# Halves straight out of PSUM, a sink as a scalar, norms in four links, a first FFN block in three pieces

## The chip, the core and the metric

The kernel runs on one core of one Trainium2 chip. The metric is the device time in microseconds of one execution of the whole program. TensorE is called PE here, VectorE DVE, ScalarE ACT, GpSimd POOL; SP issues the DMAs.

## The reference

Two layers of a backbone run over 1024 sample tokens (8 blocks of 128) and one prompt block of 128. Layer 0 mixes tokens by differential attention (8 heads, two maps of 64, 256 cached keys), layer 1 by windowed attention (16 heads in 4 groups, window 128, 256 cached keys, a sink logit per head). After each stands a projection, a norm and a SwiGLU network, D = 1024, 2816 hidden units (22 blocks of 128).

```python
# differential attention, per head
s = einsum(q, k) * HD ** -0.5
p = softmax(s, axis=-1)
a = p[:, :, 0] - lam * p[:, :, 1]
o = einsum(a, v);  o = rmsnorm(o, subln_g) * (1 - lam_init);  y = o @ w_o
# windowed attention: the sink enters maximum and sum
m = maximum(max(s), sk);  e = exp(s - m)
p = e / (sum(e) + exp(sk - m))
# around each network
x = x + gate * rmsnorm(y, g)                     # post_norm
h = rmsnorm(x, g) * (1 + scale) + shift          # pre_norm
y = (silu(h @ w_gate) * (h @ w_up)) @ w_down
```

## The kernel before

Each float32 operand of a product is split in two float32r halves, a rounded high one and the rest as low one, and a product is three matmuls (high by high, high by low, low by high). Inside each stage the program writes the order of PE, DVE, ACT and POOL by hand: what stands first in the code stands first in that engine's queue.

**Differential attention** (some 402 to 806 us) has 32 pairs of token blocks, four for each of 8 heads. The string ROUND says in which order the steps of neighbouring pairs are mixed: a token such as R111 is step R, arguments 1 and 1, of the pair one round back (last digit). S makes scores of map m for block i (two PSUM buffers), R their negative maximum (DVE), E the exponential (ACT), c and C the mix of both maps (DVE, two small instructions and one of 1280 columns), T transposes one of three groups of key blocks into the only PSUM buffer of tag "t", V copies it to SBUF (ACT), P makes the halves (POOL: `pool_round`, then a subtraction), A multiplies by V, X, B, Y bring the result out, W loads and splits a piece of the projection's weights in even rounds. DRAIN is the order after the last round.

**Windowed attention** (1960 to 2235 us) has 32 units. At its start it loads the mask and makes a bfloat16 identity; step S adds the mask by a matmul with that identity, step R takes the maximum and the minimum with the negative sink (line 1026), step E the exponential.

**The projection** (OProj; some 822 to 968 and 2237 to 2366 us) runs over 9 token blocks in the order OORDER = (0, 1, 4, 5, 2, 6, 3, 7, 8). `turn` transposes the attention's result and makes its halves; `proj` does the products, and `norms` sums squares of the result (part 0), does post_norm, the store and the sum of squares of x (part 1) and pre_norm (part 2). `step` lists what is done for which block in each step.

**The first FFN block** (968.7 to 1025.0 and 2366.1 to 2422.5 us) starts while norms still run. The products are a seven-product scheme on halves of the tokens and of the inner dimension (names B11, B21, B22, T1 to T4), made by `Halves` from pairs of token blocks. Part 0 (256 columns) is ready early; part 1 (320 columns) waits for the pairs (2, 6), (3, 7) and the prompt, made by steps listed in `late` between the products of part 0. Weights are split by `prep`: s0 and s1 are sums, h and l halves, u the last pair.

## Time and profile before

| | us |
|---|---|
| median of 3 runs | 3180.54 (3177.97 to 3180.60) |
| the profiled execution | 3179.54 |
| its span | 3177.7 |

Its mean granted clock was 0.982. Over the span PE was busy 3000.0 us (94%), DVE 2070.7 (65%), ACT 1423.8 (45%), POOL 1215.6 (38%). The chain of work that ended last is 68% PE, 13% POOL, 9% DVE, 4% ACT. These are averages over stages with different limits, so rows by stage stand below. An idle time in brackets behind a row is that of its engine before it, and the arrow names what ended it.

### The profile page before, as it was taken

Reading aid. Unit: us, or ns where it says so; the run is one execution under the profiler, and the core shown is the slowest. Engines: PE = TensorE matmul, PEld = TensorE weight load, DVE = VectorE, ACT = ScalarE, POOL = GpSimd, SP = SyncE. Lnnn points to the kernel's source line nnn. Section 1 sums busy time; section 2 is a strip of 40 time slices with the busy share of each in tenths; the row PEclk is TensorE's granted clock in tenths of the full one; section 3 lists DMA queues with packets and bytes.
Section 4 is the critical chain, followed back from the end, with each engine's and each line's share of the span. In section 5 each row is a group of like instructions: output and inputs, shape, how many; then the busy total and the mean of one; then the engine's idle time right before and its main releaser. Section 6 shows DMA issues by size and latency. Waiting matters only on the chain.

```text
span 3177.7 us, 47863 instructions
## 1 busy us (share of the span) xinstructions
PE 3000.0 (94%) x17998; PEld 2637.4 (83%) x17998; DVE 2070.7 (65%) x2849; ACT 1423.8 (45%) x2764; POOL 1215.6 (38%) x1120
## 2 busy tenths in 40 slices
PE   8999989988887999999999998999988999999999
PEld 5888777777776999999888787777768999998887
DVE  6786388888587777753786643999586633334544
ACT  6332267777554333333344323777443333333442
POOL 0453389999312444433000143666213434330000
PEclk9999999999898999999999999999999999999999
DMA  6675543332423343424865454433432322226664
GB/s 214 190 222 190 182 135 115 121 115 85 126 100 98 112 125 110 129 83 150 290 215 193 149 174 126 117 114 102 143 116 75 109 67 79 77 70 214 196 197 142
DMA packets 373807, 442.22 MB, mean 139 GB/s; under 512 B 26804, under 2 KB 295644, under 8 KB 373576
## 3 DMA queue, kind: packets, MB, share of 16 engines
q1 hardware_dynamic: 373576, 439.16, 43.9%
q8 instruction: 142, 2.33, 0.3%
q14 instruction: 89, 0.73, 0.1%
HBM read 335.71 MB, written 103.37 MB: 138 GB/s over the span
## 4 chain that ended last, share of the span: by engine, by line
PE 68%; POOL 13%; DVE 9%; ACT 4%; issue 3%; DMA 1%; SPq 1%; ACTq 0%; DVEq 0%; POOLq 0%
POOL aT L784 7%; PE guX L1516 6%; PE guX L1517 6%; PE guX L1518 6%; PE dacc L1633 6%; PE dacc L1635 6%; PE dacc L1634 6%; POOL aT L110 5%; PE qacc L556 4%; PE qacc L558 4%; PE qacc L557 4%; PE guY L1518 3%; PE guY L1516 3%; PE guY L1517 3%; PE guZ L1516 1%
## 5 line engine op out<-in xcount | busy, mean ns | idle before, releaser
L1633 PE MATMUL dacc<-fh,ahl 128*128 128x512 f32 x792 | 311.4, 393 | 2.4 <-DVE U L1552 2.4
L1635 PE MATMUL dacc<-fh,ahl 128*128 128x512 f32 x792 | 310.3, 392 | 0.0
L1634 PE MATMUL dacc<-fl,ahl 128*128 128x512 f32 x792 | 310.3, 392 | 0.0
L1549 POOL TENSOR_TENSOR sg<-sg,U 128x256 f32<-128x256 f32 x88 | 74.9, 851 | 576.2 <-ACT sg L1548 565.0
L556 PE MATMUL qacc<-whi,hh 128*128 128x512 f32 x648 | 259.3, 400 | 0.0
L558 PE MATMUL qacc<-whi,hl 128*128 128x512 f32 x648 | 254.3, 392 | 0.0
L557 PE MATMUL qacc<-wlo,hh 128*128 128x512 f32 x648 | 253.7, 391 | 0.6 <-DVE wlo L106 0.6
L617 POOL TENSOR_TENSOR qout<-t,t 128x512 f32<-128x512 f32 (+1 forms) x56 | 67.8, 1212 | 485.7 <-DVE vst L587 283.5
L784 POOL TENSOR_TENSOR aT<-a,aT 128x512 fp32r<-128x512 f32 x186 | 237.5, 1277 | 15.5
L1618 DVE TENSOR_TENSOR fl<-fraw,fh 128x1024 fp32r<-128x1024 f32 x132 | 161.7, 1225 | 118.6 <-ACT fh L1617 115.0
L744 DVE TENSOR_REDUCE nm<-S 128x1 f32<-128x1280 f32 x128 | 190.2, 1486 | 50.9 <-PE S L737 50.9
L1617 ACT CAST fh<-fraw 128x1024 fp32r<-128x1024 f32 x132 | 138.4, 1049 | 164.0 <-DMA fraw<-in_w_down_dram 157.4
L737 PE MATMUL S<-K,q 128*128 128x512 f32 (+1 forms) x768 | 184.5, 377 | 13.3 <-ACT e L749 9.2
L266 DVE SCALAR_TENSOR_TENSOR macc<-wmod,sc,macc 128x512 f32<-128x512 f32 x196 | 186.3, 994 | 0.0
L1633 PEld LDWEIGHTS dacc<-fh,ahl 128*128 128x128 f32 x792 | 148.7, 188 | 36.4 <-DVE U L1552 3.3
L1635 PEld LDWEIGHTS dacc<-fh,ahl 128*128 128x128 f32 x792 | 148.7, 188 | 33.5
L578 ACT CAST xT<-tpx 128x512 fp32r<-128x512 f32 x127 | 68.8, 591 | 240.2 <-issue 125.4
L1634 PEld LDWEIGHTS dacc<-fl,ahl 128*128 128x128 f32 x792 | 148.7, 188 | 32.8
L749 ACT ACTIVATE e<-S,nm 128x1280 f32<-128x1280 f32 x128 | 171.6, 1340 | 7.2 <-DVE nm L744 7.1
L737 PEld LDWEIGHTS S<-K,q 128*128 128x128 f32 x768 | 137.5, 193 | 44.3 <-ACT e L749 19.5
L110 POOL TENSOR_SCALAR aT<-a 128x512 fp32r<-128x512 f32 x192 | 154.2, 803 | 24.0 <-ACT a L773 24.0
L1488 DVE TENSOR_TENSOR fl<-fsum,fh 128x1024 fp32r<-128x1024 f32 x84 | 102.4, 1219 | 81.0 <-ACT fh L1486 81.0
(363 smaller groups left out, 9592.2 us busy)
## 6 DMA issues: line engine op xcount, KB each, us to landing
fraw<-in_w_down_dram SPq DMA_DIRECT2D x132, 512.0 KB
wmod<-in_w_mod_dram SPq DMA_DIRECT2D x112, 256.0 KB
araw<-a_d SPq DMA_DIRECT2D x132, 192.0 KB
...
```

Of the source, the lines that this page charges most:

```text
L110: pool.tensor_scalar(out=out, in0=in_, scalar1=1.0, scalar2=0.0, op0=ALU.mult, op1=ALU.add)
L556: pe.matmul(acc, lhsT=xh, rhs=hi[:, a, :], start=(kb == 0), stop=False)
L557: pe.matmul(acc, lhsT=xh, rhs=lo[:, a, :], start=False, stop=False)
L558: pe.matmul(acc, lhsT=xl, rhs=hi[:, a, :], start=False, stop=(kb == KB - 1))
L737: pe.matmul(S[:, j:j + n], lhsT=self.q[:, f, m, i * P:(i + 1) * P], rhs=kv[self.h][0][:, m, j:j + n], start=(f == 0), stop=(f == 1))
L784: (dve if self.last else pool).tensor_tensor(out=lo, in0=x, in1=hi.bitcast(F32), op=ALU.subtract)
L1516: pe.matmul(o, lhsT=hi[:, kb, :], rhs=xh[:, kb, :], start=(first and kb == 0), stop=False, **more)
L1517: pe.matmul(o, lhsT=hi[:, kb, :], rhs=xl[:, kb, :], start=False, stop=False, **more)
L1518: pe.matmul(o, lhsT=lo[:, kb, :], rhs=xh[:, kb, :], start=False, stop=(kb == 3), **more)
L1633: pe.matmul(acc, lhsT=ah, rhs=hi[:, cs], start=(d == 0), stop=False)
L1634: pe.matmul(acc, lhsT=ah, rhs=lo[:, cs], start=False, stop=False)
L1635: pe.matmul(acc, lhsT=al, rhs=hi[:, cs], start=False, stop=(d == NDF - 1))
```

## The change

In the differential attention the second block's third group (g = 2, i = 1, 128x256) gets its high half from ACT's copy out of PSUM and its low half from DVE, which reads PSUM too; the other five groups stay on POOL. ROUND and DRAIN are new orders. The small product of step c becomes a `tensor_scalar` with two pointer scalars. In the windowed attention the minimum with the sink becomes a `tensor_scalar`; mask and identity are made among the small parameters of layer 0. In the projection `turn` makes high halves by ACT and low halves by DVE out of PSUM, and `norms` has four links, of which the last two stand at the start of the step after the next. In the first FFN block part 1 is done as two views, 256 and 64 columns (the prompt); `Halves.first` makes two ACT copies and no DVE copies, and the order of highs and lows is new; the weights of block 1 are prepared from the `late` table, and `fetch` stands at other products. Not shown below: declarations, the pass of rooms from one stage to the next, and the column tables that follow from the views.

```diff
@@ -441,6 +444,10 @@
+        mraw = junk[:, 0:2 * P].rearrange("p (a k) -> p a k", k=P)
+        dma(out=mraw, in_=swa_mask)
+        act.copy(out=mask, in_=mraw)
+        act.copy(out=ident_b, in_=ident)
@@ -753,7 +760,7 @@
-                    dve.scalar_tensor_tensor(out=r, in0=self.s1(i), scalar=neglam, in1=r, op0=ALU.mult, op1=ALU.mult)
+                    dve.tensor_scalar(out=r, in0=r, scalar1=self.s1(i), scalar2=neglam, op0=ALU.mult, op1=ALU.mult)
@@ -767,18 +774,29 @@
-                def step_V(self, g, i):
-                    n = min(4, NKB - 4 * g)
-                    x = self.a32[i, g] = sb.tile([P, 4, P], F32, name="a32", tag="a32", bufs=2)
-                    act.copy(out=x[:, 0:n, :], in_=self.tp[i, g][:, 0:n, :])
-                def step_P(self, g, i):
+                def halves(self, g, i):
...
-                    hi, lo = [self.aT[g][:, f, 0:n, i * P:(i + 1) * P] for f in range(2)]
+                    return [self.aT[g][:, f, 0:n, i * P:(i + 1) * P] for f in range(2)]
+                def step_V(self, g, i):
+                    n = min(4, NKB - 4 * g)
+                    if (g, i) == (2, 1):
+                        act.copy(out=self.halves(g, i)[0], in_=self.tp[i, g][:, 0:n, :])
+                        return
+                    x = self.a32[i, g] = sb.tile([P, 4, P], F32, name="a32", tag="a32", bufs=2)
+                    act.copy(out=x[:, 0:n, :], in_=self.tp[i, g][:, 0:n, :])
+                def step_P(self, g, i):
+                    n = min(4, NKB - 4 * g)
+                    hi, lo = self.halves(g, i)
+                    if (g, i) == (2, 1):
+                        dve.tensor_tensor(out=lo, in0=self.tp[i, g][:, 0:n, :], in1=hi.bitcast(F32), op=ALU.subtract)
+                        return
@@ -825,16 +843,16 @@
-            ROUND = ("c001 A003 T012 A003 V202 V102 S000 R111 P213 T112 P002 A003 A003 E011 A003 P202 V012 "
...
-            DRAIN = ("c001 l1 A003 A003 V202 P213 l0 T012 V102 R111 A003 A003 P002 E011 P202 V012 A003 "
...
+            ROUND = ("T012 A003 c001 A003 R111 S000 T112 V102 C001 P102 R000 W000 A003 E011 A003 T212 S100 "
...
+            DRAIN = ("T012 A003 c001 A003 R111 T112 V102 C001 P102 A003 E011 A003 T212 V012 P012 A002 T001 "
...
@@ -980,14 +998,6 @@
-            mask = sb.tile([P, 2, P], BF16, name="mask")
...
-            act.copy(out=ident_b, in_=ident)
@@ -1023,7 +1033,7 @@
-                    dve.tensor_tensor(out=nm, in0=nm, in1=negsink[:, hs:hs + 1], op=ALU.min)
+                    dve.tensor_scalar(out=nm, in0=nm, scalar1=negsink[:, hs:hs + 1], scalar2=None, op0=ALU.min)
@@ -1301,19 +1311,20 @@
-            o32 = self.room("r1", [P, KB, P], F32, "o32")
...
+                hi, lo = oh[:, ks, :], ol[:, ks, :]
                 if self.l == 0:
-                    act.activation(out=o32[:, ks, :], in_=tp, func=AF.Copy, scale=subg)
+                    act.activation(out=hi, in_=tp, func=AF.Copy, scale=subg)
+                    dve.scalar_tensor_tensor(out=lo, in0=tp, scalar=subg, in1=hi.bitcast(F32), op0=ALU.mult,
+                                             op1=ALU.subtract)
                 else:
-                    act.copy(out=o32[:, ks, :], in_=tp)
-                pool_round(oh[:, ks, :], o32[:, ks, :])
-                dve.tensor_tensor(out=ol[:, ks, :], in0=o32[:, ks, :], in1=oh[:, ks, :].bitcast(F32), op=ALU.subtract)
+                    act.copy(out=hi, in_=tp)
+                    dve.tensor_tensor(out=lo, in0=tp, in1=hi.bitcast(F32), op=ALU.subtract)
@@ -1334,7 +1345,8 @@
-                self.ss[tb] = sumsq([x], junk)
+            elif part == 2:
+                self.ss[tb] = sumsq([self.xt[tb]], junk)
@@ -1345,9 +1357,9 @@
-                    (0, "load_x"), (1, "turn"), (3 - self.l, "load"), (-1, "norms", 0), (2, "stat", 0), (2, "stat", 1),
-                    (0, "proj", 0), *(((None, 0), (2, "scale")), ((None, 0), (2, "scale")))[self.l],
-                    (-1, "norms", 1), (-1, "norms", 2), (0, "proj", 1), (None, 1)):
+                    (-2, "norms", 2), (-2, "norms", 3), (0, "load_x"), (1, "turn"), (3 - self.l, "load"),
+                    (-1, "norms", 0), (2, "stat", 0), (2, "stat", 1), (0, "proj", 0), (None, 0), (2, "scale"),
+                    (-1, "norms", 1), (0, "proj", 1), (None, 1)):
@@ -1360,8 +1372,11 @@
+    VIEWS = ((0, 0, 256), (1, 0, 320), (1, 0, 256), (1, 256, 320))
@@ -1389,9 +1404,8 @@
-            for i, name in enumerate(("B11", "B21")):
-                act.copy(out=self.hi[name, part][:, :, c:c + a[i].shape[-1]], in_=a[i])
-                dve.tensor_copy(out=raw[:, i], in_=a[i])
+            for i in range(2):
+                act.copy(out=raw[:, i], in_=a[i])
@@ -1407,18 +1421,21 @@
+            act.copy(out=B22, in_=b[1])
             dve.tensor_tensor(out=T1, in0=b[0], in1=B11, op=ALU.subtract)
-            act.copy(out=B22, in_=b[1])
             dve.tensor_tensor(out=T, in0=B22, in1=b[0], op=ALU.subtract)
+            high("B11", B11)
+            high("B21", B21)
...
-            high("B22", B22)
             high("T2", T2)
+            low("B11", B11)
...
+            high("B22", B22)
             high("T4", T)
-            for name, x in (("B11", B11), ("B21", B21), ("T1", T1), ("T2", T2), ("B22", B22), ("T4", T)):
+            for name, x in (("B21", B21), ("T2", T2), ("T1", T1), ("B22", B22), ("T4", T)):
@@ -1471,12 +1488,16 @@
-                pool.tensor_tensor(out=s[:, 0:512], in0=A11, in1=A21, op=ALU.subtract)
-                pool.tensor_tensor(out=s[:, 512:D], in0=A12, in1=w[d, "r", "s0"][:, 512:D], op=ALU.subtract)
+                eng = pool if d else dve
+                eng.tensor_tensor(out=s[:, 0:512], in0=A11, in1=A21, op=ALU.subtract)
+                eng.tensor_tensor(out=s[:, 512:D], in0=A12, in1=w[d, "r", "s0"][:, 512:D], op=ALU.subtract)
@@ -1496,8 +1517,8 @@
+            src, c0, c1 = VIEWS[part]
...
+            xh, xl = [x[name, src][:, :, c0:c1] for x in (self.hv.hi, self.hv.lo)]
@@ -1573,14 +1596,13 @@
-                    for i, k in enumerate((0, 1, 2, 4, 3, 5, 6)):
-                        self.product(0, k, 0)
-                        for f in late[i] if i < len(late) else ():
-                            f()
-                    for k in range(7):
-                        self.product(0, k, 1)
-                        self.free(0, k)
-                        self.ahead(1, k)
+                    for view in (0, 2, 3):
+                        for i, k in enumerate((0, 1, 2, 4, 3, 5, 6)):
+                            self.product(0, k, view)
+                            if view == 3:
+                                self.free(0, k)
+                            for f in late.get((view, i), ()):
+                                f()
@@ -1785,16 +1811,13 @@
-                hooks[8, 0] = [lambda: prep("s0", "hg")]
-                hooks[8, 1] = [lambda: prep("s1", "lg")]
-                for i in range(-2, NTB):
+                hooks[8, 0] = [lambda: prep("s0", "hg", "lg")]
+                hooks[9, 0] = [lambda: prep("ha", "s1", "la")]
+                hooks[9, 1] = [lambda: prep("hb", "lb")]
+                for i in range(-2, NTB + 2):
+                    if i == NTB:
+                        f.rooms.free = [where["w0"], where["w1"], where["r1"], self.temps[0]]
                     op.step(i, hooks)
-                f.rooms.free.insert(0, self.temps[0])
-                op.norms(TB_PROMPT, 0)
-                prep("hb", "ha", "la")
-                op.norms(TB_PROMPT, 1)
-                prep("lb")
-                op.norms(TB_PROMPT, 2)
@@ -1812,11 +1835,21 @@
-                late = [[], [lambda: step(pairs[0])], [lambda: step(pairs[0], 2), lambda: f.fetch(1)],
-                        [lambda: step(pairs[1])], [lambda: step(pairs[1], 2)], [], [lambda: step(pairs[2], 2)]]
+                late = {(0, 1): [pair(0)], (0, 4): [pair(0, 2)], (0, 5): [pair(1)],
+                        (0, 6): [pair(1, 2), lambda: f.fetch(1)], (2, 1): [pair(2, 2)],
+                        (2, 3): prep("s0"), (2, 4): prep("s1"), (2, 6): prep("hg"),
+                        (3, 1): prep("lg", "ha"), (3, 3): prep("la", "hb"), (3, 5): prep("lb"),
+                        (3, 6): prep("u") + [lambda: f.fetch(2)]}
```

DVE in one even round of the differential attention (nm is the maximum, a the mixed weights, wol2 a low of the projection's weights). Before:

```order
L755 RECIPROCAL s2_4754<-s2_4754 128x1
L756 SCALAR_TENSOR_TENSOR s2_4754<-s1_all_3507,neglam_88,s2_4754 128x1
L744 TENSOR_REDUCE nm_4811<-S_4829 128x1
L761 SCALAR_TENSOR_TENSOR a_4895<-e_4819,s2_4754,e_4783 128x1280
L744 TENSOR_REDUCE nm_4905<-S_4861 128x1
L103 TENSOR_TENSOR wol2_3522<-wraw_4910,woh2_3521 128x512
L744 TENSOR_REDUCE nm_4905<-S_4914 128x1
L755 RECIPROCAL s2_4812<-s2_4812 128x1
```

The same place now:

```order
L762 RECIPROCAL s2_4730<-s2_4730 128x1
L763 TENSOR_SCALAR s2_4730<-s2_4730,s1_all_3512,neglam_88 128x1
L751 TENSOR_REDUCE nm_4823<-S_4831 128x1
L768 SCALAR_TENSOR_TENSOR a_4874<-e_4821,s2_4730,e_4782 128x1280
L751 TENSOR_REDUCE nm_4879<-S_4860 128x1
L106 TENSOR_TENSOR wol2_3527<-wraw_4882,woh2_3526 128x512
L798 TENSOR_TENSOR aT_4828<-tpa_4894,aT_4828 128x2x128
L762 RECIPROCAL s2_4824<-s2_4824 128x1
```

The subtraction of L798 is new on DVE, behind a maximum and the weights' low, and the second maximum of the next pair stands later.

DVE at the end of layer 0's projection (rs is the reciprocal root of a norm, ss its sum of squares, fl a low of weights, s1 a sum of products). Before:

```order
L1488 TENSOR_TENSOR fl_9634<-V_8154,fh_9632 128x1024
L137 RECIPROCAL rs_9637<-ss_9626 128x1
L153 SCALAR_TENSOR_TENSOR xn_9625<-oacc_9547,rs_9637,q_9619 128x512
L153 SCALAR_TENSOR_TENSOR xn_9625<-oacc_9590,rs_9637,q_9619 128x512
L1534 TENSOR_TENSOR s1_9709<-guZ_9711,s1_9709 128x256
L154 TENSOR_TENSOR K_8454<-xn_9625,K_8454 128x1024
L1488 TENSOR_TENSOR fl_9645<-K_8454,fh_9630 128x1024
L137 RECIPROCAL rs_9648<-ss_9643 128x1
```

The same place now:

```order
L133 TENSOR_TENSOR ss_9538<-ss_9538 128x1
L1492 TENSOR_TENSOR K_8395<-fraw_9413,V_8187 128x512
L1493 TENSOR_TENSOR K_8395<-fraw_9413,V_8187 128x512
L1509 TENSOR_TENSOR fl_9546<-V_8187,fh_9542 128x1024
L1556 TENSOR_TENSOR s1_9623<-guZ_9625,s1_9623 128x256
L140 RECIPROCAL rs_9549<-ss_9538 128x1
L156 SCALAR_TENSOR_TENSOR xn_9537<-oacc_9461,rs_9549,q_9531 128x512
```

The two operations of `prep`'s step s1 (L1492, L1493, a difference of weights) are new on DVE, ahead of the prompt's post_norm.

DVE at the pair (2, 6) of the first block of layer 0, which both kernels' PE waits for. Before:

```order
L1394 COPY raw_9735<-tp_n_9725 128x512
L1394 COPY raw_9735<-tp_n_9730 128x512
L1410 TENSOR_TENSOR raw_9765<-tp_n_9755,raw_9735 128x512
L1412 TENSOR_TENSOR raw_9766<-raw_9766,tp_n_9755 128x512
L1414 TENSOR_TENSOR raw_9765<-raw_9766,raw_9765 128x512
L1407 TENSOR_TENSOR T3l_9686<-raw_9766,T3h_9685 128x4x128
L1419 TENSOR_TENSOR raw_9766<-raw_9735,raw_9765 128x512
L1407 TENSOR_TENSOR B11l_9676<-raw_9735,B11h_9675 128x4x128
```

The same place now:

```order
L1425 TENSOR_TENSOR raw_9705<-tp_n_9695,raw_9649 128x512
L1500 TENSOR_TENSOR fhl_9566<-V_8187,fhl_9566 128x512
L1426 TENSOR_TENSOR raw_9706<-raw_9706,tp_n_9695 128x512
L1430 TENSOR_TENSOR raw_9705<-raw_9706,raw_9705 128x512
L1421 TENSOR_TENSOR B11l_9590<-raw_9649,B11h_9589 128x4x128
```

The two copies are gone from DVE, and the low of B11 stands four places earlier within its pair.

## Rows read from the trace of the kernel before

**Rows 1.** Busy time by stretch: us, busy time (instructions) of PE, PEld, DVE, ACT, POOL, PE's clock, DMA share, GB/s
```profile
420.00:790.00 370.00, 332.60 (x2200) 289.94 (x2200) 321.86 (x305) 263.29 (x476) 355.48 (x348) 1.00 0.35 111
968.70:1025.00 56.30, 35.72 (x209) 33.59 (x208) 41.23 (x60) 25.06 (x48) 11.17 (x9) 0.82 0.23 72
1966.00:2225.00 259.00, 240.41 (x1629) 199.43 (x1629) 234.04 (x463) 195.50 (x463) 161.91 (x183) 0.98 0.40 116
2366.00:2422.50 56.50, 33.63 (x209) 31.81 (x209) 42.39 (x61) 24.75 (x48) 11.07 (x9) 0.82 0.25 78
```

**Rows 2.** The chain of waits of 485 to 720 us, by line
```profile
by line: POOL aT L784 61.1%; POOL aT L110 35.8%; issue 3.4%
```

**Rows 3.** Lines of DVE, 420 to 790: count | busy us, mean ns | idle before
```profile
L756 DVE SCALAR_TENSOR_TENSOR s<-s_all,neglam,s 128x1 f32<-128x1 f32 x58 | 21.3, 368 | 2.1
...
L755 DVE RECIPROCAL s<-s 128x1 f32<-128x1 f32 x58 | 8.8, 151 | 0.0
```

**Rows 4.** Timeline of POOL, differential attention: start us, us, instruction
```profile
503.05 0.41 POOL L110 TENSOR_SCALAR aT<-a 128x256 fp32r<-128x256 f32 x1
...
503.54 0.74 POOL L784 TENSOR_TENSOR aT<-a,aT 128x256 fp32r<-128x256 f32 x1
```

**Rows 5.** Timeline of the loop of the scores, the same stretch
```profile
503.59 1.34 ACT L749 ACTIVATE e<-S,nm 128x1280 f32<-128x1280 f32 x1
...
503.84 1.49 DVE L744 TENSOR_REDUCE nm<-S 128x1 f32<-128x1280 f32 x1 [0.74 <-PE S L737]
...
505.07 1.44 PE L737 MATMUL S<-K,q 128*128 128x512 f32 x6
```

**Rows 6.** Lines of DVE, windowed attention, 1966 to 2225
```profile
L1026 DVE TENSOR_TENSOR nm<-nm,negsink 128x1 f32<-128x1 f32 x128 | 46.4, 362 | 4.4
```

**Rows 7.** Lines of PE, windowed attention, 1966 to 2225
```profile
L1014 PE MATMUL S<-K,q 128*128 128x256 f32 x252 | 59.1, 316 | 18.4 <-ACT e L1029 18.3
```

**Rows 8.** Timeline of PE, start of the windowed attention
```profile
1965.15 0.26 PE L1020 MATMUL S<-mask,ident_b 128*128 128x128 bf16 x1 [4.67 <-ACT mask L987]
```

**Rows 9.** Lines of PE, projection of layer 0, 806 to 968
```profile
L1324 PE MATMUL oacc<-woh,oh 128*128 128x512 f32 x143 | 60.8, 425 | 4.5 <-DVE xn L153 4.5
...
L1386 PE MATMUL tp_n<-ident,xn 128*128 128x128 f32 x32 | 5.1, 311 | 3.1 <-DVE raw L1394 3.1
```

**Rows 10.** Lines of PE, projection of layer 1, 2237 to 2366
```profile
L1324 PE MATMUL oacc<-woh,oh 128*128 128x512 f32 x144 | 59.1, 410 | 5.2 <-DVE xn L153 5.2
```

**Rows 11.** Timeline of PE, projection and first block of layer 0
```profile
881.91 0.28 PE L939 MATMUL av<-pr 128*128 128x128 f32 x1
882.02 0.28 PE L940 MATMUL av<-pr 128*128 128x128 f32 x1
...
970.49 0.28 PE L1517 MATMUL guX<-B11l,fh 128*128 128x256 f32 x1
970.61 0.28 PE L1518 MATMUL guX<-B11h,fl 128*128 128x256 f32 x1
...
1009.37 0.63 PE L1517 MATMUL guX<-B11l,fh 128*128 128x320 f32 x1 [8.84 <-DVE B11l L1407]
```

**Rows 12.** Lines of DVE, 951 to 1010, shapes apart
```profile
L153 DVE SCALAR_TENSOR_TENSOR xn<-oacc,rs,q 128x512 f32<-128x512 f32 x6 | 4.2, 747 | 0.1
L145 DVE SCALAR_TENSOR_TENSOR xn<-K,rs,bc 128x1024 f32<-128x1024 f32 x3 | 3.9, 1284 | 0.1
...
L154 DVE TENSOR_TENSOR K<-xn,K 128x1024 f32<-128x1024 f32 x3 | 3.7, 1221 | 0.1
...
L1407 DVE TENSOR_TENSOR T2l<-raw,T2h 128x512 fp32r<-128x512 f32 x2 | 1.4, 680 | 0.0
...
L1488 DVE TENSOR_TENSOR fl<-V,fh 128x1024 fp32r<-128x1024 f32 x1 | 1.2, 1226 | 3.3 <-ACT fh L1486 3.3
...
L137 DVE RECIPROCAL rs<-ss 128x1 f32<-128x1 f32 x6 | 1.0, 162 | 4.4 <-ACT ss L135 4.4
```

**Rows 13.** Timeline of DVE, end of the projection of layer 0
```profile
953.74 0.16 DVE L137 RECIPROCAL rs<-ss 128x1 f32<-128x1 f32 x1 [0.36 <-ACT ss L135]
```

57 lines of the change are left out of this document (33 added, 24 removed), and 6 rows, old and new, of the table DRAIN.

## The prediction, made before the changed kernel was run

> **What bounds the kernel now.** I read the profile in this order: busy time by stretch, the chain of waits inside the slowest-looking stretch, then the lines and timelines of the engine that the chain names. TensorE (PE) is busy 94% of the whole span, so a gain can only come from stretches where it isn't. Four of the stretches that the change touches are such [rows 1]. In the differential attention PE is busy 332.6 of 370 us, VectorE (DVE) 321.9, but GpSimd (POOL) 355.5, 96%. The chain of waits there is 97% POOL, all of it the rounding and the subtraction that make the halves of the transposed weights [rows 2]. So POOL sets the end there. In the window attention PE is busy 93%, and what it lacks is a wait for the exponentials [rows 1, 7]. In the two first FFN blocks PE is busy 35.7 of 56.3 us and 33.6 of 56.5, at a granted clock of 0.82 [rows 1]; the reader is to see there the one wait of 8.84 us for DVE [rows 11]. At the end of each projection PE waits for DVE's norms and copies: 4.5, 3.1 and 5.2 us [rows 9, 10].
>
> **Differential attention.** In the 370 us stand 58 reciprocals, two a round [rows 3]: 29 rounds of 12.76 us. By the same division a round keeps POOL busy 12.26, PE 11.47 and DVE 11.10 [rows 1]. The change takes one of the six halving steps off POOL (another moves by a round and stays on it): a rounding of 0.41 and a subtraction of 0.74 at 128x256 [rows 4], together 1.15. POOL's floor becomes 12.76 - 1.15 = 11.6. ACT makes its copy as before, now the high half itself, at no new cost. DVE gains one 128x256 subtraction, about 0.4 as an estimate (a 128x512 one takes 0.68 [rows 12]), and its two small products per round go from a three-operand form at 0.368 to a form with two pointer scalars. That form isn't in the trace; the nearest row is the 128x1 reciprocal on the line before, which never waits for POOL, at 0.151 [rows 3]. So DVE stays at 11.10 + 0.4 - 2 x 0.2 = 11.1; if the new form is no cheaper, 11.5. The loop of the scores through two PSUM buffers is not in the way: 1.44 for the matmuls, 1.49 for the maximum, and 1.48 from the exponential's start to the next matmuls [rows 5], 4.4 twice a round, 8.8. POOL at 11.6 and PE at 11.47 now stand close, in an order by hand, and PE also gets the transposes earlier, so neither will be hidden by the other to the last tenth. I take 11.9: 0.86 less, in 31 full rounds 27 us. Bounds: 11.6 (36 us) and nothing (0); below nothing too, by the one-bank wait under rival F.
> The drain after the last round has its own new order. The first two statistics of the projection stand later in it, the third earlier, and its last subtractions were DVE's already. Each statistic is ACT work of short pieces beside PE's last products; I allow 2 us of loss, 0 to 5.
>
> **Window attention.** The minimum with the sink takes 0.362 on average over 128 instructions, 46.4 us of DVE [rows 6], for one element per partition; the reciprocal of one element takes 0.151 [rows 3]. With the sink as a pointer scalar I price it by that row: 4 x 0.21 = 0.84 less DVE per unit of 259 / 32 = 8.1 us [rows 1], 27 in all. It stands between the maximum and the exponential for which PE waits, 18.3 us in all [rows 7], and PE's own work is 240.4 of the 259. So the gain ends at 18.3 whatever DVE saves. The other cover of that wait is the maximum itself, which stays. I take 11, with bounds 0 and 18.3.
> The mask and the small identity are now made in layer 0, from DMA and two ACT copies, at a point where the QKV product is running. PE's wait of 4.67 for the mask at the start of the attention [rows 8] goes; what is late next is the first maximum and exponential, which were behind that same matmul. I take 4, bounds 0 and 4.7. The DMA and the copies in layer 0 are of 128x256 and 128x128; they are covered by PE's QKV products, and without cover they would cost under 1 us.
> First the row: a one-element subtraction-like instruction with two inputs in SBUF takes 0.362, one with a single input 0.151 [rows 3, 6], beside a POOL that is busy. The Trainium skill, "SBUF — State Buffer", section "Who interferes with whom", speaks for this change in its first half (a DVE instruction with two SBUF inputs contends with GpSimd's reads) and against it in its second: it counts tensor_scalar among the operations that can enter a two-port mode and then wait for GpSimd's whole instruction. By that second half the new form would wait as the old one did; that is rival B.
>
> **Projection.** The halves of its left operand come straight out of PSUM: POOL's rounding goes off the path, DVE's subtraction stays. The norms of one block are cut into four links over two steps, so that DVE no longer sits behind ACT's sum of squares between post- and pre-norm. That wait is 4.4 in the three norm pairs after 951 us [rows 12]. The PE waits that can go are 4.5 for a post-norm (a PSUM bank), 3.1 for a copy out of the transposes' bank, and 5.2 for a post-norm in layer 1 [rows 9, 10]: 12.8. The copies move from DVE to ACT, which is busy under two thirds here, and the links make more norms meet at one point of DVE's queue, so I take 9, bounds 0 and 12.8; with the clock's dips behind those waits up to 20.
>
> **The first FFN block.** Its second part waits for halves of five token blocks, the last of which are normed after the projection's end. DVE is the engine waited for. I walk its queue from the reciprocal of a late post-norm, at 953.74, to the product that restarts PE at 1009.37 [rows 11, 13], 55.6 us. After the change the product that PE restarts with is 256 columns wide and needs only the pairs of blocks, not the prompt's. Ahead of it DVE has, by rows of before:
> three post-norms, 4.2 + 3.7 and the reciprocals' 0.7, 8.6; three pre-norms, 3.9 and 3.7 for an addition of the same shape, with the rest of the reciprocals, 8.0; lows of the weights, three of 1.2, 3.6; the first sum of weights that POOL made before, two of 0.68, 1.4; the last low of the weights, 0.7; three or four sums of squares and of products, some 1.5 [rows 12];
> eleven operations for the first pair, where there were thirteen (the two copies go to ACT), spaced 0.63 as estimated from the 0.68 with its overlap: 6.9; four operations of the second pair to the first low needed, 2.5; waits for ACT, of which 4.4 and 3.3 stand in the trace [rows 12] and about half stays: 3.7.
> Together 36.9, so PE restarts 18.7 us earlier. Then it has more to do than before. Before, from 1009.37 to the block's end at 1025 it took 15.7 us for one pass of 84 matmuls at 320 columns. Now it is a pass of 84 at 256 columns, spaced 0.12 (970.49 and 970.61), 10.1; and a pass of 84 at 64 columns. No matmul of 64 columns stands in this trace's stretch; the nearest has 128 columns, spaced 0.11 (881.91 and 882.02) [rows 11], so 9.2; bounds 4.6 (half, by columns) and 10.1 (as 256). Transposes, waits for their two banks and the half clock after the wait I take at 5.2: the block lost 20.6 to waits before, 8.84 of it here. That is 24.5, 8.8 more than before. Net 18.7 - 8.8 = 9.9 per layer, 20 for both. Bounds: 0, if the second pair's lows are late by ten more us, and 18.7 per layer, 37, if none of the 8.8 is paid. The weights' preparation for the next block now stands behind the 64-column products; it is covered by them, and if it isn't, each low of 1.2 that is late costs itself. The DMAs of the next blocks' weights move on SP's queue from the third product to the first pass's end and the block's end; the DMA engines are busy 23% there [rows 1], and nothing of this block waits for them.
> The Trainium skill, "VectorE: DVE Perf Modes", section "The TRN2 errata — SBUF-src ops pay a fixed extra latency per instruction", gives a matmul max(60, 6 + columns) cycles at 2.4 GHz. By that formula 64 columns take 0.029 and the pass 2.4, an estimate from that page, and the sum would be 13 to 14 us lower. The row speaks against it: 128 columns stand 0.11 apart [rows 11], where the formula has 0.056.
>
> **Sum.** -27 + 2 - 11 - 4 - 9 - 20 = -69. The profiled run took 3179.54, so 3110.5; the median of the runs shown is 1.0 above the profiled run, so 3111 to 3112; I say 3111.
>
> **Rivals.**
> A, the forecast: 3111, own range 3092 to 3130. 0.42.
> B, the scalar form waits for POOL as the old form did: the 11 of the window attention stay (DVE's 11.5 in the other attention doesn't bind), 3122. For it: POOL is busy 162 of 259 us there [rows 1]. Against: the reciprocal, one input, shows 0.151 beside a POOL that is 96% busy [rows 1, 3]. 0.08.
> C, a new wait takes POOL's place in the round, PE in the order by hand or DVE: the round ends at 12.6 (gain 5 instead of 27), and the window attention gives nothing: 3111 + 22 + 11 = 3144. For it: PE 11.47 and DVE 11.1 lie within 10% of the bound. Against: each has over 0.4 of room. 0.13.
> D, more is hidden than I allow: the round at 11.6 (-9), the window attention at PE's floor (-7), all 12.8 in the projections (-4), the first block near its bound (-16): 3075 with all four, 3090 with half. For it: these are the floors of busy time. 0.15.
> E, DVE's queue is no shorter ahead of the product, since norms that are two steps late meet the pairs: first blocks and projections give nothing, 3111 + 29 = 3140. 0.15.
> No change, the moves hidden everywhere: 3180. 0.02.
> F, slower. One PSUM bank holds the transposes. Before, an ACT copy freed it each time; now for one group of six DVE's subtraction must also have read it, and that stands in DVE's order behind a maximum of 1.49 [rows 5] and, in even rounds, a low of the projection's weights. If PE's next transpose waits for all of it and nothing else is ready, that is 1.49 and about 0.7 for the operation and the weights' share, and the loss repeats through the following transposes: 2.7 a round gives 14.6, and 31 x 2.7 = 84 over 3111, 3195. It decides from a round of 11.9 + 69 / 31 = 14.1 on. Against: PE has score and value products between the transposes. 0.05.
>
> **How the numbers follow.** The time is A's. The range holds A, B, C and E and most of D: 3072 to 3147. What a measurement can tell from no change is 0.2%, 6.4 us; faster are A to E, 0.93; same 0.02; slower F, 0.05.
>
> **What would show it.** In the changed kernel's profile: 58 reciprocals of the differential attention in some 345 us, POOL still above 93% there; the small products near 0.15 to 0.2; the minimum with the sink the same, and PE's wait for the exponentials near 7 instead of 18.3; no wait for the mask; PE restarting in the first block some 37 us after the late post-norm, and 64-column matmuls 0.11 apart; the first block at about 46 us. It is wrong if a round stays above 12.5, if the sink's line stays above 0.3, or if the 256-column pass still waits 8 us for DVE.

## The result and the profile after

The changed kernel took 3129.68 us (median of 4 runs, 3127.23 to 3130.93), the kernel before 3179.6 beside it: ratio 0.9843, 95% interval 0.9826 to 0.986. That is 50 us less; 69 were forecast. The profiled execution of the changed kernel has a span of 3128.1.

Busy time by stretch of the changed kernel, same columns as [rows 1]: differential attention, windowed attention, projection of layer 0 and of layer 1, first FFN block of layer 0 and of layer 1, then two pieces of layer 0's first block (256 columns, 64 columns), the products behind it, and the 64-column piece of layer 1.

```profile
420.00:760.00 340.00, 331.42 (x2217) 292.03 (x2216) 310.12 (x336) 271.05 (x480) 327.90 (x292) 1.00 0.38 121
1925.00:2171.00 246.00, 235.09 (x1622) 197.18 (x1620) 214.58 (x460) 195.19 (x459) 160.39 (x181) 0.99 0.44 127
794.80:921.50 126.70, 120.20 (x596) 98.85 (x595) 93.30 (x164) 77.19 (x232) 3.46 (x2) 0.99 0.41 128
2184.70:2308.40 123.70, 121.00 (x596) 98.38 (x595) 83.55 (x140) 57.73 (x123) 2.94 (x2) 1.00 0.45 140
921.40:985.40 64.00, 48.52 (x294) 45.76 (x292) 39.18 (x60) 31.31 (x65) 10.10 (x9) 0.75 0.25 82
2308.40:2371.70 63.30, 47.53 (x294) 45.05 (x292) 38.43 (x60) 31.36 (x65) 9.39 (x9) 0.77 0.26 85
948.00:970.20 22.20, 16.88 (x93) 16.06 (x94) 13.87 (x23) 8.90 (x22) 7.20 (x5) 0.65 0.10 29
970.20:985.40 15.20, 14.90 (x87) 14.76 (x85) 4.27 (x6) 3.65 (x9) 1.05 (x2) 0.61 0.26 77
985.40:991.00 5.60, 5.60 (x25) 5.60 (x26) 2.71 (x4) 0.37 (x1) 4.88 (x5) 0.53 0.31 84
2356.20:2371.70 15.50, 15.20 (x87) 15.06 (x86) 4.28 (x6) 3.59 (x9) 1.08 (x3) 0.60 0.29 87
```

Read against [rows 1]: in the differential attention PE is now at 331.4 of 340 (97.5%) where it was at 90%, and POOL still at 96%. Both first blocks, by contrast, are longer, 64.0 and 63.3 instead of 56.3 and 56.5, at a lower clock (0.75 and 0.77 instead of 0.82), and PE is busy 13 to 14 us longer in each. The seventh line is the 256-column piece, the eighth the 64-column piece: PE is busy 14.9 of 15.2 us there, at 0.61. Layer 1's 64-column piece, the last line, reads the same: 15.2 of 15.5, at 0.60.

The projection of layer 0 before, for the comparison with the third line:

```profile
826.30:968.70 142.40, 128.99 (x595) 105.42 (x594) 102.73 (x173) 76.08 (x230) 19.36 (x19) 0.92 0.42 131
```

Its clock went from 0.92 to 0.99; PE's busy time fell by 8.8 us, its idle time by 6.9.

The stages in both traces, each from PE's first matmul of one kind to the last of that kind or the first of the next:

| stage | before | after | difference | forecast |
|---|---|---|---|---|
| differential attention, first to last score | 407.5 | 373.6 | -33.9 | -27 |
| drain and way to the projection's first product | 28.6 | 31.1 | +2.5 | +2 |
| projections (layer 0, layer 1) | 142.2, 126.9 | 126.6, 123.6 | -15.7, -3.3 | -9 together |
| first blocks (layer 0, layer 1) | 56.3, 56.4 | 64.0, 63.3 | +7.7, +6.9 | -20 together with the next row |
| the 24 matmuls behind them | 3.2, 3.2 | 5.6, 5.4 | +2.4, +2.2 | in the row above |
| windowed attention, first to last score | 263.1 | 246.4 | -16.7 | -15 |
| everything else | | | -1.7 | 0 |
| sum | | | -49.6 | -69 |

The two attentions alone gave 50.6 us, the whole difference. Projections and first blocks (with the matmuls behind them), from which the forecast expected 29 us, cancel: together they cost 0.2 us.

The small instructions of DVE in the changed kernel: duration in ns, minimum, median and maximum, then first and last start. The first is the sink's minimum, the second the small product of the differential attention, the third the reciprocal ahead of it.

```profile
L1036 DVE TENSOR_SCALAR nm<-nm,negsink x128: 212/214/217, 1925.9 to 2171.5; 128x1 f32<-128x1 f32 x128
```

```profile
L763 DVE TENSOR_SCALAR s<-s,s_all,neglam x64: 272/273/277, 401.9 to 768.7; 128x1 f32<-128x1 f32 x64
```

```profile
L762 DVE RECIPROCAL s<-s x64: 144/151/155, 401.7 to 768.5; 128x1 f32<-128x1 f32 x64
```

Both new forms answer [rows 3, 6], where the old ones took 368 and 362 on average. The averages hide what went. The same view of the old minimum with the sink:

```profile
L1026 DVE TENSOR_TENSOR nm<-nm,negsink x128: 158/236/1124, 1966.2 to 2223.7; 128x1 f32<-128x1 f32 x128
```

At its shortest the old form took 158 ns, less than the new one. But 46 of the 128 took over 300 ns; each of these began while a POOL instruction ran and ended within 0.26 us behind the end of one. The new forms never wait so: the spread is 5 ns, beside a POOL that is busy 65% and 96%. They are not as cheap as the reciprocal: one pointer scalar makes 214, two make 273.

PE's wait for the exponentials in the windowed attention, which answers [rows 7]:

```profile
L1024 PE MATMUL S<-K,q 128*128 128x256 f32 x254 | 58.4, 311 | 10.4 <-ACT e L1039 10.4
```

It fell from 18.3 to 10.4, not to 7. And there is no wait for the mask where [rows 8] has 4.67:

```profile
1924.90 0.23 PE L1030 MATMUL S<-mask,ident_b 128*128 128x128 bf16 x1
```

PE in the first block of layer 0, which answers [rows 11]: the restart, the 64-column pass where its clock falls, and the first product of the next block.

```profile
949.49 0.58 PE L1538 MATMUL guX<-B11l,fh 128*128 128x256 f32 x1 [0.88 <-DVE B11l L1421]
...
970.32 0.28 PE L1539 MATMUL guX<-B11h,fl 128*128 128x64 f32 x1
970.43 0.28 PE L1537 MATMUL guX<-B11h,fh 128*128 128x64 f32 x1
...
973.34 0.28 PE L1539 MATMUL guX<-T2h,fl 128*128 128x64 f32 x1
973.45 0.30 PE L1537 MATMUL guX<-T2h,fh 128*128 128x64 f32 x1
973.56 0.40 PE L1538 MATMUL guX<-T2l,fh 128*128 128x64 f32 x1
973.77 0.40 PE L1539 MATMUL guX<-T2h,fl 128*128 128x64 f32 x1
973.99 0.40 PE L1537 MATMUL guX<-T2h,fh 128*128 128x64 f32 x1
...
985.74 0.41 PE L1538 MATMUL guX<-B11l,fh 128*128 128x256 f32 x1
985.95 0.41 PE L1539 MATMUL guX<-B11h,fl 128*128 128x256 f32 x1
```

On DVE the walk of this block begins here, the row that answers [rows 13]:

```profile
909.00 0.16 DVE L140 RECIPROCAL rs<-ss 128x1 f32<-128x1 f32 x1 [0.36 <-ACT ss L138]
```

The wait that ends last before the restart is 0.88, where it was 8.84. The 64-column matmuls stand 0.11 apart, as the forecast had it, until 973.45; then, with no wait in between, they stand 0.21 apart, and stay so to the end of the pass and through the next block's first products (256 columns 0.21 apart instead of 0.12).

On DVE's way from the reciprocal to there, two waits for ACT's sums of squares stand between post- and pre-norm:

```profile
921.81 0.16 DVE L140 RECIPROCAL rs<-ss 128x1 f32<-128x1 f32 x1 [1.61 <-ACT ss L138]
934.25 0.16 DVE L140 RECIPROCAL rs<-ss 128x1 f32<-128x1 f32 x1 [3.04 <-ACT ss L138]
```

### The profile page after: what moved, and what is told of

The parts are those of the page before. It is cut to its first block, busy times and chain, and to the rows that moved or that the text cites. A ratio compares the mean times of both kernels' runs of the same rounds, so it can differ in the third digit from the quotient of the medians.

```text
span 3128.1 us, 48178 instructions
## 1 busy us (share of the span) xinstructions
PE 3011.3 (96%) x18166; PEld 2655.0 (85%) x18166; DVE 2014.9 (64%) x2870; ACT 1447.0 (46%) x2798; POOL 1143.1 (37%) x1021
## 5 line engine op out<-in xcount | busy, mean ns | idle before, releaser
L1571 POOL TENSOR_TENSOR sg<-sg,U 128x256 f32<-128x256 f32 (+2 forms) x90 | 76.0, 844 | 639.3 <-ACT sg L1570 533.8
L802 POOL TENSOR_TENSOR aT<-a,aT 128x512 fp32r<-128x512 f32 (+1 forms) x155 | 199.1, 1284 | 12.9
L744 PE MATMUL S<-K,q 128*128 128x512 f32 (+1 forms) x768 | 183.3, 375 | 12.4 <-ACT e L756 11.7
L744 PEld LDWEIGHTS S<-K,q 128*128 128x128 f32 x768 | 137.4, 192 | 40.4 <-ACT e L756 15.5
L113 POOL TENSOR_SCALAR aT<-a 128x512 fp32r<-128x512 f32 (+1 forms) x160 | 157.4, 984 | 21.8 <-ACT a L791 21.8
```

The source lines that it names most:

```text
L744: pe.matmul(S[:, j:j + n], lhsT=self.q[:, f, m, i * P:(i + 1) * P], rhs=kv[self.h][0][:, m, j:j + n], start=(f == 0), stop=(f == 1))
L802: (dve if self.last else pool).tensor_tensor(out=lo, in0=x, in1=hi.bitcast(F32), op=ALU.subtract)
```

## Experiments

The reasons to be told apart. Theory: the first blocks lose because PE's clock falls to 1.2 GHz, half of full, within the 64-column pass; that and the extra passes eat what the projections give. Rivals: the norms that moved into the block make it long; the clock falls because of PE's waits before. For the attentions: it is the halves off POOL, or the new order, or the small scalar forms.

**One pass of 320 columns again.**

```diff
-                    for view in (0, 2, 3):
+                    for view in (0, 1):
...
-                        (0, 6): [pair(1, 2), lambda: f.fetch(1)], (2, 1): [pair(2, 2)],
+                        (0, 6): [pair(1, 2), lambda: f.fetch(1), pair(2, 2)],
+                        (1, 0): prep("s0"), (1, 1): prep("s1", "hg"), (1, 2): prep("lg", "ha"),
+                        (1, 3): prep("la", "hb"), (1, 4): prep("lb"),
+                        (1, 6): prep("u") + [lambda: f.fetch(2)]}
```

> The changed kernel with the second part of the first FFN block done again in one pass of 320 columns behind the prompt's halves, all else as changed (the weights of block 1 are prepared in that pass). Theory (the 64-column pass is what costs: it took 15.2 us, most of it at a granted clock of half, and the next two products 2.4 more): PE restarts some 11 us later per layer, then has one pass of 12.4 to 15.7 instead of 22 and 15, and no half clock after it; each first block ends about 10 us earlier, the whole at about 3110. Rival (the early restart of the 256-column piece is a gain, and the block is long for another reason, DVE's norms that moved into it): the wait for the prompt comes back, the blocks end 5 to 10 us later each, the whole at 3140 to 3150.

Measured: 3102.04 us, ratio to before 0.9754 (0.974 to 0.9769). This is 28 us under the changed kernel, and the shortest time of all kernels here. The first blocks in it, of both layers:

```profile
922.80:973.30 50.50, 33.87 (x209) 31.03 (x208) 36.58 (x55) 29.77 (x56) 9.16 (x7) 0.80 0.24 79
2292.20:2344.70 52.50, 33.93 (x210) 31.65 (x209) 38.38 (x57) 30.80 (x61) 8.81 (x7) 0.80 0.30 98
```

And the waits that came back:

```profile
952.21 0.64 PE L1537 MATMUL guX<-B11h,fh 128*128 128x320 f32 x1 [3.33 <-ACT B11h L1418]
958.40 0.63 PE L1538 MATMUL guX<-B11l,fh 128*128 128x320 f32 x1 [5.55 <-DVE B11l L1421]
```

PE waits longer here, 3.33 us for ACT and 5.55 for DVE ahead of the pass, and the blocks are still 13.5 and 10.8 us shorter than in three pieces (50.5 against 64.0, 52.5 against 63.3). Together with the matmuls behind them, back at 3.2 us each, that accounts for the 28. The restart that the three pieces bring forward, from 35.6 to 28.1 us behind the block's start, is worth less than the extra passes cost. The norms that moved into the block are the same in both kernels, so they aren't the cause. Done in one pass, the blocks are also 5.8 and 3.9 us shorter than before the change.

**The third piece 128 columns wide.**

```diff
-    VIEWS = ((0, 0, 256), (1, 0, 320), (1, 0, 256), (1, 256, 320))
+    VIEWS = ((0, 0, 256), (1, 0, 320), (1, 0, 256), (1, 192, 320))
...
```

> The changed kernel with the third piece 128 columns wide (the prompt's 64 and 64 that the piece before has already done; these results are made twice and stored once). It tells what lowers the clock in that piece. Theory one, the narrow products themselves: with 128 columns at the same spacing of 0.11 the clock stays at full, the pass takes 9.3 instead of 15.2 and the next two products are 2.4 faster, 8 us per layer, the whole at about 3113. Theory two, PE's idle waits in the 30 us before: the clock falls as before, the pass takes 15 again, the whole stays at 3130.

Measured: 3115.96 (3106.52 to 3117.9), ratio 0.98 (0.9783 to 0.9816), 14 us less than the changed kernel for more columns of work. The pass in the profiled execution, layer 0 and layer 1:

```profile
968.50:978.40 9.90, 9.55 (x86) 9.40 (x85) 4.41 (x6) 3.92 (x9) 1.19 (x3) 1.00 0.27 84
2340.70:2350.60 9.90, 9.54 (x87) 9.41 (x85) 4.41 (x6) 3.80 (x9) 1.19 (x2) 1.00 0.43 125
```

```profile
969.80 0.27 PE L1537 MATMUL guZ<-B21h,fh 128*128 128x128 f32 x1
969.91 0.27 PE L1538 MATMUL guZ<-B21l,fh 128*128 128x128 f32 x1
```

Twice the columns at the same spacing of 0.11, and the granted clock stays at 1.00: the pass takes 9.9 instead of 15.2. The waits before it are nearly the same: in layer 0 1.19, 0.88, 2.41 and 1.29 us from the restart on, where the changed kernel has 1.19, 0.88, 3.11 and 1.30. So it was the 64-column products and not the waits before them that cost the clock. The profiled execution took 3106.52 and the other three 3114.70 to 3117.90, so the same kernel was run again.

> The kernel with the third piece 128 columns wide, once more: its profiled execution took 3106.5, its other three 3114.7 to 3117.9. Theory (in the slower ones the clock falls elsewhere, in one of the first blocks or the stages ahead, while the 128-column pass keeps it): a profile near 3116 shows half-clock stretches that the first didn't have, and the pass at 9.3 to 9.9 us again. Rival (the pass itself loses the clock in those executions): the pass takes 15 in at least one layer.

Measured: 3112.18 (two runs). Start of the windowed attention in the first profile and, in the next fence, in this one, followed by the 128-column pass of layer 0 and of layer 1 in this one:

```profile
1912.00:1930.00 18.00, 13.35 (x94) 10.82 (x94) 12.70 (x31) 12.21 (x30) 4.42 (x5) 1.00 0.93 273
```

```profile
1912.00:1930.00 18.00, 14.73 (x78) 11.86 (x77) 8.47 (x20) 9.35 (x22) 1.88 (x2) 0.72 0.83 244
...
971.90:981.80 9.90, 9.54 (x87) 9.40 (x85) 4.41 (x6) 3.90 (x9) 1.19 (x2) 1.00 0.27 84
2347.40:2357.30 9.90, 9.54 (x86) 9.40 (x85) 4.41 (x6) 3.82 (x9) 1.20 (x3) 1.00 0.43 121
```

The pass keeps its clock and takes 9.9 us again, in both layers. The 7 us between the two profiles lie elsewhere: 3.2 in the windowed attention (247.1 from first to last score, 243.9 in the first profile), which starts with a stretch of half clock here and not there; 3.2 in layer 0's first block ahead of the pass; the rest in smaller differences.

**The second part cut at 128 columns.**

```diff
-    VIEWS = ((0, 0, 256), (1, 0, 320), (1, 0, 256), (1, 256, 320))
+    VIEWS = ((0, 0, 256), (1, 0, 320), (1, 0, 128), (1, 128, 320))
...
+                        (0, 6): [lambda: f.fetch(1)], (2, 1): [pair(1, 2)],
+                        (2, 3): [pair(2, 2)],
...
```

> The changed kernel with the second part of the first block cut otherwise: 128 columns that need only the pair (2, 6), then 192 that need the pair (3, 7) and the prompt. No piece is narrower than 128. Theory (products of 128 columns and more keep the clock, and the first piece of 9.3 us fills most of the 11.8 us that PE waits in the one-pass kernel, for some 7 us more of products): 0 to 8 us under the one pass, 3094 to 3102. Rival (DVE's order with the sums of two pieces delays the last halves, and each pass pays its banks' waits): 3105 to 3115.

Measured: 3111.84 (3110.64 to 3113.53). The rival held: 10 us over the one pass. In its trace the 128-column piece runs among waits, the longest 3.73 us for ACT and 1.83 for DVE in layer 0, and behind these twelve of its matmuls take 2.6 us instead of 1.34, at half clock (0.73 over this piece, 0.57 in layer 1). So in these runs 128 columns kept the clock where PE didn't wait between them, and not among waits.

**The projection and first block alone.** The kernel before with all hunks of the diff from `turn` on and nothing else; both attentions, their orders and the mask are as before.

```diff
+                    act.copy(out=hi, in_=tp)
+                    dve.tensor_tensor(out=lo, in0=tp, in1=hi.bitcast(F32), op=ALU.subtract)
...
+                    (-2, "norms", 2), (-2, "norms", 3), (0, "load_x"), (1, "turn"), (3 - self.l, "load"),
...
+                    for view in (0, 2, 3):
```

> The kernel before with the projection's and the first block's changes alone (halves out of PSUM, norms in four links, three pieces); both attentions and the mask as before. Theory (the projections gain some 19 us, the first blocks and the products behind them lose as much): 3175 to 3185, no change that can be told. Rival (the forecast's sizes, hidden in the changed kernel by its other parts): 29 us less, 3151.

Measured: 3180.86 (10 runs), ratio 0.9998 (0.9988 to 1.0007). The two halves of this edit cancel: from its trace, the projections are 131.6 and 123.2 us instead of 142.2 and 126.9, and the first blocks 60.7 and 63.8 instead of 56.3 and 56.4, with 2.7 and 2.0 more behind them. Its 64-column passes, of layer 0 and of layer 1:

```profile
1006.70:1021.60 14.90, 14.60 (x86) 14.46 (x86) 4.27 (x6) 3.71 (x9) 1.09 (x3) 0.63 0.26 75
2410.50:2426.20 15.70, 15.40 (x86) 15.26 (x85) 4.27 (x6) 3.56 (x9) 1.08 (x3) 0.59 0.29 86
```

They lose the clock as the two of the changed kernel do: four passes of four.

**The norms in three links again**, in the one-pass kernel.

```diff
-                    (-2, "norms", 2), (-2, "norms", 3), (0, "load_x"), (1, "turn"), (3 - self.l, "load"),
+                    (0, "load_x"), (1, "turn"), (3 - self.l, "load"), (-1, "norms", 0), (2, "stat", 0), (2, "stat", 1),
...
+                    (-1, "norms", 1), (-1, "norms", 2), (0, "proj", 1), (None, 1)):
```

> The kernel of the one pass of 320 columns (3102) with the norms in three links again: pre-norm right behind post-norm, and the weights' preparation at its old places; the projection's halves still come straight out of PSUM. Theory (the links take DVE's wait for the sum of squares out of the row of norms and keep the clock at full in the projection): the wait of 4.5 in layer 0 and of 5.2 in layer 1 come back, and norms end later; 8 to 15 us more, 3110 to 3117. Rival (the projection's gain is that of the halves without POOL): 3102 to 3105.

Measured: 3111.34, 9 us over the one-pass kernel. The projection of layer 0 with three links, and (next fence) with four:

```profile
794.00:928.70 134.70, 125.28 (x595) 102.72 (x594) 94.33 (x166) 78.04 (x234) 3.46 (x2) 0.95 0.41 124
```

```profile
794.00:922.90 128.90, 122.83 (x595) 100.76 (x594) 95.59 (x167) 77.94 (x234) 3.45 (x2) 0.97 0.43 130
```

With three links this projection takes 5.8 us more, part of it at a lower clock (0.95 against 0.97), and the block behind it 4.6 more (55.1 against 50.5). Layer 0's projection with four links and halves straight out of PSUM took 126.4 to 129.7 us in the six profiles here that have both, so the 134.7 lies outside their spread. This run also has the weights' preparation back at its old places; what of the difference is the links' own is not shown.

**The projection's halves by way of POOL again**, in the one-pass kernel: `turn` as in the kernel before.

```diff
-                    act.copy(out=hi, in_=tp)
-                    dve.tensor_tensor(out=lo, in0=tp, in1=hi.bitcast(F32), op=ALU.subtract)
+                    act.copy(out=o32[:, ks, :], in_=tp)
+                pool_round(oh[:, ks, :], o32[:, ks, :])
+                dve.tensor_tensor(out=ol[:, ks, :], in0=o32[:, ks, :], in1=oh[:, ks, :].bitcast(F32), op=ALU.subtract)
...
```

> The kernel of the one pass of 320 columns (3102) with the projection's halves made the old way: an ACT copy, POOL's rounding, DVE's subtraction from SBUF. Theory (the halves are made a step ahead of their products, so POOL's rounding is covered, and what the projection gained came from the links): 3102 to 3106. Rival (DVE's instructions with two SBUF inputs wait for POOL again and PE waits for them): 3110 or more.

Measured: 3105.91 (3104.06 to 3107.74), 3.9 us over the one-pass kernel: at the theory's upper end. By the two profiles the projections themselves take the same (129.5 and 122.8 against 128.9 and 123.2), so POOL's rounding is covered there. What is longer is the way from the last score of the windowed attention to layer 1's first product, 16.8 against 14.1; 2.8 more stand ahead of the first attention, where the two kernels are alike.

**The differential attention alone.** The kernel before with the three hunks on step c, on the halves and on the two orders.

```diff
+                    if (g, i) == (2, 1):
+                        act.copy(out=self.halves(g, i)[0], in_=self.tp[i, g][:, 0:n, :])
+                        return
...
+            ROUND = ("T012 A003 c001 A003 R111 S000 T112 V102 C001 P102 R000 W000 A003 E011 A003 T212 S100 "
```

> The kernel before with the differential attention's change alone (new orders, one group's halves out of PSUM, the pointer scalars). Theory (it gives what the two traces show, 34 us to the last score, 4 more in the drain, and 6 lost again before the projection's first product): 3147 to 3149. Rival (the projection's norms caused that late start, or hide part of it): 3141 or less. Round of 11.65 us in both.

Measured: 3144.97, ratio 0.9892 (0.9877 to 0.9907): 35 us less, between the theory's 3147 and the rival's 3141. By its trace the drain's way to the projection is 29.5 us here, against 31.1 in the changed kernel. Layer 0's projection, whose own code is that of before, takes 137.5 us instead of 142.2. The stretch reads as in the changed kernel, and its chain of waits by line (485 to 720 us) follows:

```profile
420.00:760.00 340.00, 331.46 (x2216) 292.25 (x2217) 310.04 (x338) 270.73 (x481) 327.82 (x293) 1.00 0.38 121
```

```profile
by line: POOL aT L795 55.3%; POOL aT L110 42.1%; issue 3.1%; POOLq L110 0.1%
```

POOL still owns 97% of the chain, with PE busy 97.5% beside it.

**The same with all six halving steps on POOL.**

```diff
-                    if (g, i) == (2, 1):
-                        act.copy(out=self.halves(g, i)[0], in_=self.tp[i, g][:, 0:n, :])
-                        return
...
-                    if (g, i) == (2, 1):
-                        dve.tensor_tensor(out=lo, in0=self.tp[i, g][:, 0:n, :], in1=hi.bitcast(F32), op=ALU.subtract)
-                        return
```

> The kernel with the differential attention's change alone (3145), with all six halving steps on POOL again under the new order. Theory (POOL sets the round, and the step off POOL is the gain): POOL busy 12.3 us a round, round 12.3 to 12.6, 20 to 30 us more, 3165 to 3175. Rival (the new order is the gain): 3145 to 3150.

Measured: 3184.6, ratio 1.0012 (1.0002 to 1.0022): 40 us more than with the step off POOL. Of the 4 over the kernel before, 2.4 stand ahead of the attention. Its stretch and its chain of waits by line:

```profile
420.00:790.00 370.00, 331.80 (x2172) 287.54 (x2172) 308.44 (x303) 264.45 (x471) 355.65 (x344) 1.00 0.35 110
```

```profile
by line: POOL aT L789 51.2%; POOL aT L110 46.1%; issue 3.4%
```

POOL is at 355.65 of 370 as in [rows 1] and owns 97% of the chain as in [rows 2]. The new order by itself gives the attention nothing (409.8 us from first to last score, 407.5 before); under it, the step off POOL gives it all. The step off POOL under the old order was not run. The cost of its return was more than the 20 to 30 of the theory, since the round goes back to 12.8 and not to the 12.3 of POOL's busy time. Layer 0's projection takes 138.8 us here, against 142.2 before and 137.5 with the step off POOL: what it gained ahead of its own changes came mostly with the new orders.

**The small product in its three-operand form again.**

```diff
-                    dve.tensor_scalar(out=r, in0=r, scalar1=self.s1(i), scalar2=neglam, op0=ALU.mult, op1=ALU.mult)
+                    dve.scalar_tensor_tensor(out=r, in0=self.s1(i), scalar=neglam, in1=r, op0=ALU.mult, op1=ALU.mult)
```

> The kernel with the differential attention's change alone (3145), with the two small products a round in the three-operand form again (0.37 on average instead of 0.273). Theory (PE, at 97.5% busy, sets the round; DVE at 91% has room): 3143 to 3148, no change that can be told. Rival (the small product stands in the loop from exponential to the halves and delays it): 0.2 a round and its longest waits, 6 us or more, 3151 or more.

Measured: 3144.39 against 3144.97: no difference that can be told. By the traces the attention is if anything shorter with the old form (370.4 us between the starts of first and last score, 373.4 with the new): DVE has room there.

**The sink as a scalar alone**, in the kernel before.

```diff
-                    dve.tensor_tensor(out=nm, in0=nm, in1=negsink[:, hs:hs + 1], op=ALU.min)
+                    dve.tensor_scalar(out=nm, in0=nm, scalar1=negsink[:, hs:hs + 1], scalar2=None, op0=ALU.min)
```

> The kernel before with the sink as a pointer scalar in the windowed attention alone; the mask stays where it was. Theory (a form without contention at 0.214 instead of 0.362): the units take 12 us less, 3168. Rival (the wait for the exponentials is set by the maximum; the gain seen in the changed kernel came from the mask's move): 3177 or more.

Measured: 3166.58, ratio 0.9955 (0.994 to 0.997). From first to last score the attention takes 251.0 instead of 263.1. So 12 of the 16.7 us are the scalar's. The mask's share, 4.6, is what is left; no run has the mask's move alone, but the wait for it [rows 8] is still 4.54 us in this trace and gone in the changed kernel's.

**The statistics earlier in the drain**, in the one-pass kernel.

```diff
-                     "A001 V111 X002 P111 V211 A001 B002 P211 A001 Y002 s00 s01 A001 A001 A001 A001 A001 "
+                     "P001 T101 C011 V201 P201 T011 s00 A002 A002 T111 V101 s01 P101 A002 A002 T211 V011 P011 A001 "
+                     "A001 V111 X002 P111 V211 s10 n0 A001 B002 P211 A001 Y002 A001 A001 A001 A001 A001 "
```

> The kernel of the one pass of 320 columns (3102) with the first three statistics of the projection and the first scale moved back into the drain's earlier part, where ACT stands idle 0.6 to 2.6 us between copies. Theory (the projection's first transposes wait 5.4 us for that scale, 1.5 before the change): 3 to 5 us less, 3097 to 3099. Rival (the statistics then delay the copies out of PSUM by as much): 3102 or more.

Measured: 3109.07, 7 us more; the rival. PE's waits in the drain of this kernel, by line, two rows of it, and (next fence) the same two in the one-pass kernel:

```profile
L1319 PE MATMUL tp_o<-ident,V 128*128 128x128 f32 x13 | 2.3, 332 | 4.8 <-issue 4.8
L824 PE MATMUL tpo<-ident,oT 128*128 128x128 f32 x6 | 1.6, 350 | 4.8 <-DVE aT L798 4.3 <-ACT oT L818 0.5
```

```profile
L1319 PE MATMUL tp_o<-ident,V 128*128 128x128 f32 x16 | 3.9, 428 | 6.7 <-DVE V L1289 5.4 <-DVE oh L1323 1.4
L824 PE MATMUL tpo<-ident,oT 128*128 128x128 f32 x6 | 1.5, 340 | 1.6 <-ACT oT L818 1.6
```

The wait did not go. In the first row 4.8 of the 6.7 us still stand; they are put down as issue, but the transposes start 0.1 us behind the end of DVE's scale of their block. In the second 4.3 us come new, from DVE's subtraction out of the one PSUM bank, which stands in DVE's queue behind the scale that was moved ahead of it. Some 2 us more of the 7 stand ahead of the attention, where the two kernels are alike.

## Why the prediction came out as it did

The total lies in the stated range, at the upper end of the likeliest case's own, and the direction was right. That it lies there is in part luck: the first blocks cost 19 us where 20 less were forecast, a miss of 39, and the attentions and projections, which gave 18 us more than forecast, covered nearly half of it. One step failed, and several sizes were off.

- **The step that failed: the 64-column pass.** "No matmul of 64 columns stands in this trace's stretch; the nearest has 128 columns, spaced 0.11, so 9.2". The spacing was right at full clock. What the step left out is the clock: the pass took 15.2 us, beyond the stated bound of 10.1, and the 24 matmuls behind it 2.4 more. Shown by the four passes of 64 columns, all at 0.59 to 0.63, and the four of 128, 9.9 us at full clock. With it fails the net gain of three pieces: the first block, forecast at about 46 us, took 64.0, and one pass took 50.5.
- **The 256-column pass.** Forecast 10.1 and 5.2 for transposes, bank waits and half clock; it took 20.7 us from the restart to the first 64-column product, at a clock of 0.65. Together with the restart itself, 40.5 us behind the reciprocal (949.49 after 909.00, the post_norm that answers [rows 13]) where 36.9 was forecast, layer 0's block ends 76.4 us behind that reciprocal where it was 71.3 before: 5.1 more where 9.9 less was forecast, 3.6 of the miss by the restart, 5.4 by this pass, 6.0 by the next.
- **The walk of DVE's queue** was right to 10%, and with it the claim that the wait goes. Its operations came as listed; the 3.6 that it missed are nearly all waits for ACT, 7.1 us where 3.7 were allowed. The four links did not take away the wait for the sum of squares there: 1.60, 1.61 and 3.04 us in the last three norm pairs. And the value of an early restart was overrated: the one-pass kernel waits for DVE and is faster.
- **The projections** were undersized: -19 instead of -9. The forecast named the cause of the difference ("with the clock's dips behind those waits up to 20"): the clock of layer 0's stretch went from 0.92 to 0.99, and 8.8 of its 15.7 us are PE's shorter busy time. With the projection's and the block's own changes alone layer 0's projection gave 10.6 us; 4.7 came with the differential attention's change, which the forecast didn't count here. The kernel with three links puts 5.8 us on the links with the weights' preparation; the kernel with POOL's rounding puts nothing on the halves within the projections, but 2.7 on the way into layer 1's.
- **Differential attention**: 33.9 instead of 27. The step off POOL is all of it under the new order, as argued. The round became 11.7 (the 64 reciprocals now stand in 366.8 us), 1.1 less, where the forecast allowed 0.86 of the step's 1.15. POOL still sets it by the chain above; PE at 97.5% stands close behind. Two readings were off without harm. The 11.6 called POOL's floor is the old round less the step; POOL's busy time less the step is 12.26 - 1.15 = 11.1, and it came to 11.3. And 0.74 for the subtraction is one row of [rows 4]; the 58 of its shape in 420 to 790 us took 1.256 on average. Of the larger step that went, part came back: the 128x512 subtractions left on POOL take 1.43 instead of 1.30, the roundings 1.14 instead of 1.00. The two small products cost 0.273 instead of the forecast's 0.151, and it made no difference.
- **Windowed attention**: 16.7 instead of 15. The scalar gave 12 (forecast 11), the mask 4.6 (forecast 4). The form costs 0.214 and not 0.151, and PE still waits 10.4 for the exponentials: the maximum ahead of them stays.
- **Rivals.** B is refuted: the scalar form doesn't wait. The Trainium skill, "SBUF — State Buffer", section "Who interferes with whom", counts tensor_scalar among the operations that can take the port pair shared with GpSimd, when their operands meet the conditions for it; here 128 of them took 212 to 217 ns beside a busy POOL, so on one element per partition it doesn't show. Its other half, that two SBUF inputs contend with GpSimd's reads, fits what the change removed: 362 on average and up to 1124 before, 214 now. C didn't come: in the kernel with this attention's change alone the chain is still POOL's. E's result came (projections and first blocks together gave nothing), not by its mechanism: DVE's queue did get shorter (40.5 us from the reciprocal to the restart, 55.6 before). F didn't come: PE has other work beside the one bank in a round; its waits for that subtraction sum to 0.6 us over 420 to 760 us. In the drain, with the statistics moved, that wait did appear, 4.3 us.
- **The spacing.** By the formula of the Trainium skill, "VectorE: DVE Perf Modes", section "The TRN2 errata — SBUF-src ops pay a fixed extra latency per instruction", a 64-column matmul would take 0.029; the rows show 0.11, as the row of 128 columns in [rows 11] had it.

Open is what lowered the clock in the 20 us before the 64-column pass (0.65 in the 256-column piece). It goes with PE's waits there, as before the change, but no kernel here took these waits away. Open too are the step off POOL under the old order, and how the projections' gain divides between links, weights' preparation and orders.
